# Small slots of the second expert stage: float32 weights without a split, products in separate columns of the array, loads in whole rows

## The chip, the cores and the metric

The kernel runs on one core of a Trainium2 chip. The metric is device time in microseconds from the first to the last instruction of that core. Three runs of the kernel before gave 2158.07 us in the median.

## What is computed

Two transformer blocks follow each other on 1024 tokens of 1024 features, in float32. Each has a mixer (a short convolution in the first, an mLSTM and a pooling branch in the second) and a layer of experts behind it. In the first block 16 experts take their 128 best tokens each. In the second block every token picks a group and, in it, two of eight experts; there are 32 experts of inner width 512. The change is about the products of these experts:

```python
def run_block(args):
    tok, e = args
    xb = hf[jnp.minimum(tok, n_tok - 1)]
    a = xb @ w_gate[e]                                # 1024 x 512
    b = xb @ w_up[e]                                  # 1024 x 512
    return (jax.nn.silu(a) * b) @ w_down[e]           # 512 x 1024
...
out = (out.reshape(n_slots, dm).astype(jnp.float32) * slot_gate[:, None]).astype(h.dtype)
y = jnp.zeros((n_tok, dm), h.dtype).at[slot_tok].add(out, mode='drop')
```

A final norm follows the second block.

## The kernel before

**Order of the kernel.** `block1` runs the first mixer, the routing and 16 experts; `block2` runs the second mixer, the routing, 32 expert slots and the final norm. In the profile the first expert stage lies at about 480 to 1030 us, the second mixer behind it, the second expert stage at about 1490 to 2131 us, and the final norm at the end.

**Slots of the second stage.** The routing sorts the 32 experts by their number of tokens into slots of four sizes: four slots of two blocks of 128 tokens (PAIRS_AT, positions 5, 10, 15, 20), twelve of 128 (the first three and WHOLE_AT), six of 64 (HALF_AT, positions 26 to 31) and ten of 32 (QUARTER_AT: 6, 7, 11, 12, 16, 17, 21, 22, 24, 25). The last two kinds are called small here; they have an entry "m", their number of tokens. Which expert a slot holds is read from memory by the SP queue when its weights are loaded.

**Order of the work.** `unit_order` gives, for slot after slot, the products of gate and up, the transposition of the next slot's tokens (xT), the products of the last slot's down, and the transposition of this slot's hidden values (hT). `queue_experts` loads the weights in the same order.

**Loads.** `Loader` runs chunks of 1 MB, [128, 4, 512] in float32, on the SP queue, four in flight, into 14 ring buffers (two rings of two, and two pools of five). A chunk covers 512 rows and 512 columns of a weight, by `chunk_src`. Where a weight is 512 wide (gate and up of the second stage) the pieces of 512 columns are whole rows of 2 KB; where it is 1024 wide (all weights of the first stage, down of the second) they are halves of rows.

**Splits.** TensorE multiplies in fp32r with operands split into hi and lo: ScalarE copies a rounded hi (L188) and VectorE subtracts it (L189). `ahead` in `run_experts` does so for half a chunk at a time (128 x 1024 numbers), into five split buffers, in the order of use. A chunk's ring buffer is free once its second half is split.

**Products of large slots** are three fp32r products for each block of 128 features (`mm3`, L196 to L198). **Small slots** turn their tokens so that hi and lo of xT lie side by side in the stationary columns (2m of them) and go once over the weights' hi (L554) and once over their lo (L555); the two halves of the result are added by `whole` (L560 and L561). Down's weights aren't split for small slots: hT is float32, and `product_few` multiplies the raw chunk (L552), one column half after the other. All these results begin at PSUM partition 0. The row product with the gate and the modulation row is L681; GpSimd then scatters the rows with an adding DMA (L515) to `acc_d`. GpSimd also gathers the tokens (L509).

**The end.** Slot 31's rows are not scattered: `keep_rows` keeps them, and the final norm adds them. Behind slot 30's scatter `load_sums` reads the sums back (L1336), and the final norm runs on them (L1402, L1415).

Of the kernel before, what the change touches and what calls it, by code (L numbers as in the profile page):

```python
# [21 lines left out]
P = 128  # L22
# [15 lines left out]
# positions of the slots where each kind starts, its tokens  # L38
# [12 lines left out]
class Loader:  # L51
    """Runs weight chunks from DRAM into rings of buffers, in the order of their use."""
# [13 lines left out]
    def drop_pools(self):  # L66
        """All but the first two."""
        del self.pools[2:]
# [24 lines left out]
            # what else wants the DMA engines doesn't wait behind more than this many loads  # L93
# [6 lines left out]

    def take(self, key):
        k, v, p = self.ready.popleft()
        assert k == key, (k, key)
        self.held[key] = p
        return v

    def done(self, key, keep=False):
        """keep: the buffer becomes the caller's, who takes it from the ring."""
        p = self.held.pop(key)
        if not keep:  # L110
            p[3] -= 1
            self.pump()
# [7 lines left out]
def kernel(ctx, tc, a, out):  # L120
# [13 lines left out]
    def psum_pools(stack, **bufs):  # L134
        """PSUM's 8 banks: mm and p tiles take two each, aux tiles one."""
# [9 lines left out]
    def keep_warm(n):  # L145
        """Products of constants while the tensor engine would wait for long, for its clock falls to half when idle."""
# [58 lines left out]
    C = {}  # L205

    def routing_consts():
# [10 lines left out]
        # before[s, t] = 1 where s < t  # L218
# [4 lines left out]
        # same[r, c] = 1 where r and c are the same modulo 16; prev: and r < c  # L223
# [6 lines left out]
        # the first token of each row's tile  # L230
# [15 lines left out]
    def turned_rows(pool, srcs):  # L246
        """Vectors as columns, in PSUM."""
# [8 lines left out]
    class Ada:  # L256
        """Columns of silu(c) @ ada_w + ada_b, 512 at a time; chunks of the weights run ahead."""
# [75 lines left out]
    def first_units(hls, ps, hT, ready):  # L333
        """The first few blocks of columns, by half of the tokens and feature block as they get ready."""
# [13 lines left out]
    def proj_T(hl, hT, n=P):  # L348
        """[n features, tokens] of h @ w for one block of columns; hT: its halves by token."""
# [15 lines left out]
    def mix_out(stack, b, y, parts, wo0, w_key, resid, g_row, mods, router, n_log, L, after_wo0, bias=None, ready=lambda tt: None, beside=lambda tt: None):  # L365
        """parts: y's feature blocks, those that get ready last behind; ready(tt): what is left to do for the last part;
        beside(tt): what else is to be done before the next tile;
        mods: scale, weight and shift of the second norm.
        L: the router's logits by token, (x * rstd * (1 + scale) * weight + shift) @ router with the columns' factors
        taken into the router and the tokens' left to the end."""  # L370
# [64 lines left out]
        for tt in range(NT):  # L435
# [29 lines left out]
            # the last tiles go ahead of the weights that follow  # L465
# [11 lines left out]
            if tt == NT - 1:  # L477
                # off the vector engine, which goes on with the routing
# [15 lines left out]
    class Experts:  # L494
# [34 lines left out]
        def transposed_few(self, x, n, tag, m):  # L529
            """Up to 64 tokens; xT: hi and lo side by side, for one pass over the weights' hi and one over their lo;  # L530
            hT: float32, for weights that are not split."""
# [3 lines left out]
            src = ps[:, :n * m].rearrange("p (k c) -> p k c", k=n)  # L535
# [12 lines left out]
        def product_few(self, sT, w, ps, ks, last):  # L548
            ps = ps[:sT.shape[2]]
            for i, k in enumerate(ks):  # L550
                if sT.dtype == F32:
                    nc.tensor.matmul(ps, sT[:, k], w[:, i], start=k == 0, stop=k == last)  # L552
                else:
                    nc.tensor.matmul(ps, sT[:, k], w[:, 0, i], start=k == 0, stop=False)  # L554
                    nc.tensor.matmul(ps, sT[:, k], w[:, 1, i], start=False, stop=k == last)  # L555

        def whole(self, t, p, m):
            """The sum of the halves that hi and lo give, kept in t."""
            t = t[:m]
            nc.scalar.copy(t, p[m:2 * m])  # L560
            nc.vector.tensor_tensor(t, p[:m], t, op=OP.add)  # L561
            return t
# [1384 lines left out]
```

## Time and profile before

| | us |
|---|---|
| three runs | 2157.3, 2158.07, 2159.38 |
| span of the profiled execution | 2157.5 |
| TensorE busy | 2007.7 (93%) |
| VectorE busy | 1653.2 (77%) |
| ScalarE busy | 1147.8 (53%) |
| GpSimd busy | 350.4 (16%) |

The profiled execution's own time is its span, from the first to the last instruction; nothing beside the span is listed for it. Busy time is the union of an engine's instructions. Consecutive matmuls overlap in the records, so a gap between two of them shows as idle only where it is longer than that overlap. The DMA share is the mean of the core's 16 DMA engines and can read slightly above 1.

### The profile page before, as it was taken

To read this page: it belongs to the slowest core of one execution; us is meant where nothing else is said; L and a number is where in the kernel's file an instruction comes from. 1 tells how busy PE (TensorE), PEld (TensorE's weight loads), DVE (VectorE), ACT (ScalarE), POOL (GpSimd) and SP (SyncE) were. 2 spreads that over 40 slices of the span, in tenths; PEclk is the share of its full clock that TensorE was granted. 3 is DMA by queue.
4 is the path that set the end of the run, shared out by engine and by line. 5 is a ranking of instruction groups with operands and counts; after the bars stand their busy time and mean duration, and the time that the engine had idled before them with its cause. 6 is when DMAs were issued, how large, how long until landed. Compare 5 with 4: busy or idle time off the path is not lost.

```text
span 2157.5 us, 25812 instructions
## 1 busy us (share of the span) xinstructions
PE 2007.7 (93%) x9192; PEld 1543.5 (72%) x9192; DVE 1653.2 (77%) x2073; ACT 1147.8 (53%) x1568; POOL 350.4 (16%) x300
## 2 busy tenths in 40 slices
PE   4999999949999999999699998996999999999997
PEld 3788878827888888888477877785886757575553
DVE  6699965458999999999562456777977787778886
ACT  4311122227777777777552444233766565656664
POOL 1054420040101010000100001004112121112210
PEclk7999999969999999999899999997999999999999
DMA  9467645389999999999502001538999999999996
GB/s 312 157 236 263 243 141 204 106 309 351 366 380 372 380 372 380 373 380 365 153 1 84 15 30 49 205 137 284 387 321 329 325 341 325 333 332 330 360 371 231
DMA packets 300799, 573.59 MB, mean 266 GB/s; under 512 B 30311, under 2 KB 53575, under 8 KB 300668
## 3 DMA queue, kind: packets, MB, share of 16 engines
q1 hardware_dynamic: 281116, 511.78, 66.2%
q0 software_dynamic: 19168, 59.46, 9.5%
q8 instruction: 73, 1.20, 0.2%
q10 hardware_dynamic: 384, 0.68, 0.1%
q14 instruction: 58, 0.48, 0.1%
HBM read 534.12 MB, written 42.66 MB: 267 GB/s over the span
## 4 chain that ended last, share of the span: by engine, by line
PE 85%; DVE 8%; ACT 3%; issue 2%; DMA 2%; POOL 0%; SPq 0%; DVEq 0%; ACTq 0%; POOLq 0%
PE mm L196 21%; PE mm L197 21%; PE mm L198 21%; PE mm L552 5%; PE aux L525 2%; PE mm L554 2%; PE mm L555 2%; DVE hl L189 2%; PE half L198 1%; PE half L196 1%; PE half L197 1%; PE aux L414 1%; ACT hl L188 1%; PE aux L1528 1%; DVE adacc L298 1%
## 5 line engine op out<-in xcount | busy, mean ns | idle before, releaser
L189 DVE TENSOR_TENSOR hl<-raw,hl 128x1024 fp32r<-128x1024 f32 x729 | 869.6, 1232 | 134.6 <-ACT hl L188 124.3
L188 ACT CAST hl<-raw 128x1024 fp32r<-128x1024 f32 x740 | 757.9, 1053 | 264.8 <-PE mm L198 226.9
L196 PE MATMUL mm<-hl,xT 128*128 128x512 f32 x832 | 330.9, 398 | 0.3 <-ACT xT L192 0.3
L198 PE MATMUL mm<-hl,xT 128*128 128x512 f32 x832 | 327.6, 394 | 0.0
L197 PE MATMUL mm<-hl,xT 128*128 128x512 f32 x832 | 327.6, 394 | 0.0
L196 PE MATMUL mm<-hT,hl 128*128 128x512 f32 x448 | 180.2, 402 | 8.2 <-ACT hT L819 5.9
L198 PEld LDWEIGHTS mm<-hl,xT 128*128 128x128 f32 x832 | 156.5, 188 | 36.7 <-DVE xT L193 0.7
L196 PEld LDWEIGHTS mm<-hl,xT 128*128 128x128 f32 x832 | 156.5, 188 | 35.5 <-ACT xT L192 0.8
L197 PEld LDWEIGHTS mm<-hl,xT 128*128 128x128 f32 x832 | 156.7, 188 | 34.6
L197 PE MATMUL mm<-hT,hl 128*128 128x512 f32 x448 | 178.6, 399 | 1.6 <-DVE hT L820 1.6
L198 PE MATMUL mm<-hT,hl 128*128 128x512 f32 x448 | 176.5, 394 | 0.0
L196 PE MATMUL mm<-hl,hT 128*128 128x512 f32 x416 | 168.4, 405 | 3.4 <-ACT hl L188 3.2
L197 PE MATMUL mm<-hl,hT 128*128 128x512 f32 x416 | 166.1, 399 | 3.8 <-DVE hl L189 3.8
L198 PE MATMUL mm<-hl,hT 128*128 128x512 f32 x416 | 165.8, 398 | 0.9 <-DVE hT L193 0.9
L552 PE MATMUL mm<-raw,hT 128*32 128x512 f32 (+1 forms) x256 | 113.0, 594 | 0.5 <-ACT hT L538 0.5
L515 POOL DMA_INDIRECT acc_d<-yo,idx x35 | 60.6, 1732 | 281.2 <-DVE yo L681 233.7
L196 PEld LDWEIGHTS mm<-hT,hl 128*128 128x128 f32 x448 | 85.7, 191 | 28.6 <-ACT hT L819 6.4
L554 PE MATMUL mm<-hl,xT 128*64 128x512 f32 (+1 forms) x256 | 101.6, 397 | 0.0
L555 PE MATMUL mm<-hl,xT 128*64 128x512 f32 (+1 forms) x256 | 101.0, 395 | 0.4 <-DVE hl L189 0.4
L298 DVE SCALAR_TENSOR_TENSOR adacc<-adaw,ccol,adacc 128x512 f32<-128x512 f32 x142 | 100.0, 770 | 0.0
L197 PEld LDWEIGHTS mm<-hT,hl 128*128 128x128 f32 x448 | 85.5, 191 | 19.3 <-DVE hT L820 2.4
L198 PEld LDWEIGHTS mm<-hT,hl 128*128 128x128 f32 x448 | 85.3, 190 | 19.1
(481 smaller groups left out, 3129.6 us busy)
## 6 DMA issues: line engine op xcount, KB each, us to landing
raw<-in_moe_w_gate_dram SPq DMA_DIRECT2D x64, 1024.0 KB
raw<-in_moe_w_up_dram SPq DMA_DIRECT2D x64, 1024.0 KB
raw<-in_moe_w_down_dram SPq DMA_DIRECT2D x64, 1024.0 KB
raw<-in_w_expert_gate_dram SPq DMA_DIRECT2D x64, 1024.0 KB
raw<-in_w_expert_down_dram SPq DMA_DIRECT2D x63, 1024.0 KB
raw<-in_w_expert_up_dram SPq DMA_DIRECT2D x62, 1024.0 KB
adaw<-in_ada_w_dram SPq DMA_DIRECT2D x47, 1024.0 KB
raw<-in_sc_w_in_dram SPq DMA_DIRECT2D x9, 1024.0 KB
```

The source lines that it names most:

```text
L188: nc.scalar.copy(hl[:, 0], raw)
L189: lo.tensor_tensor(hl[:, 1], raw, hl[:, 0].bitcast(F32), op=OP.subtract)
L196: nc.tensor.matmul(o, s_hi, m_hi, start=start, stop=False)
L197: nc.tensor.matmul(o, s_hi, m_lo, start=False, stop=False)
L198: nc.tensor.matmul(o, s_lo, m_hi, start=False, stop=stop)
L298: nc.vector.scalar_tensor_tensor(acc[kk % 2], w[:, k], c, add, op0=OP.mult, op1=OP.add)
L414: nc.tensor.matmul(o, xT[:, k], rsc[:, k], start=k == 0, stop=k == KC - 1)
L515: nc.gpsimd.indirect_dma_start(out=self.acc, out_offset=bass.IndirectOffsetOnAxis(ap=idx[:m], axis=0), in_=y[:m], in_offset=None, compute_ ...
L525: nc.tensor.transpose(ps[:, i * P:(i + 1) * P], x[:, k * P:(k + 1) * P], ident)
L552: nc.tensor.matmul(ps, sT[:, k], w[:, i], start=k == 0, stop=k == last)
L554: nc.tensor.matmul(ps, sT[:, k], w[:, 0, i], start=k == 0, stop=False)
L555: nc.tensor.matmul(ps, sT[:, k], w[:, 1, i], start=False, stop=k == last)
```

## The change

- For small slots of the second stage no weight is split any more. xT is float32 like hT, and gate and up are float32 products on the raw chunks. A chunk of gate stays in its ring buffer until the chunk of up with the same rows is there; `queue_experts` loads the two alternately.
- `product_few` places the products in the array. The first of its weights goes to the PSUM partitions from 0, the second to those from 64. For slots of 32 tokens odd feature blocks go 32 partitions higher than even ones. Its two weights are up and gate, or the two column halves of down.
- `few_sums` brings the parts together: for 64 tokens it copies the upper half down, for 32 it adds the two sums of each weight.
- `few` is the new path of small slots. It calls `ahead` for the weights of the next large slots, whose chunks may come later in the queue than the small ones'; `Loader.take` finds a chunk by its key, and `ahead` goes on only if that load has been issued.
- `chunk_src` loads whole rows in both expert stages: [128, 4, 512] for weights 512 wide, [128, 2, 1024] for weights 1024 wide. Large slots multiply the two column halves of a block of 128 features one after the other where the weight is 1024 wide; a pair's down then takes two PSUM tiles at once.

The diff also takes out comments, which are left out here.

```diff
+    def is_ready(self, key):
+        return any(r[0] == key for r in self.ready)
     def take(self, key):
-        k, v, p = self.ready.popleft()
-        assert k == key, (k, key)
+        i, (_, v, p) = next((i, r) for i, r in enumerate(self.ready) if r[0] == key)
+        del self.ready[i]
...
         def transposed_few(self, x, n, tag, m):
...
-            if tag == "hT":
-                t = self.tile("hT32", [n, P // 2], 1)[:, :, :m]
-                nc.scalar.copy(t, src)
-                return t
-            t = self.tile(tag, [2, n, P], self.wide, F32R).rearrange("p a b c -> p (a b) c")[:, :n, :2 * m]
-            nc.scalar.copy(t[:, :, 0:m], src)
-            nc.vector.tensor_tensor(t[:, :, m:], src, t[:, :, 0:m].bitcast(F32), op=OP.subtract)
+            t = self.tile(tag, [2, n, P], self.wide)[:, 0, :, :m]
+            nc.scalar.copy(t, ps[:, :n * m].rearrange("p (k c) -> p k c", k=n))
...
+        def product_few(self, sT, ws, ps, k, last):
+            m = sT.shape[2]
+            split = P // 2 // m
+            for i, w in enumerate(ws):
+                at = i * (P // 2) + k % split * m
+                nc.tensor.matmul(ps[at:at + m], sT[:, k], w, start=k < split, stop=k > last - split)
+        def few_sums(self, ps, m, outs):
+            if m == P // 2:
+                for i, o in enumerate(outs):
+                    if o is not None:
+                        nc.scalar.copy(o, ps[i * m:(i + 1) * m])
+                return
+            t = self.tile("whole", [512], 1)
+            for at in (P // 2, 0):
+                nc.scalar.copy(t[at:at + m], ps[at + m:at + 2 * m])
+            for i in (1, 0):
+                at = i * (P // 2)
+                nc.vector.tensor_tensor(outs[i], ps[at:at + m], t[at:at + m], op=OP.add)
...
+        def few(i, kind, c):
...
+            raw = ld.take(key)
+            if key[2] == "g":
+                gate_raw = key, raw
+                if ci == 0:
+                    ps = mm_ps()[:, 0]
+                return
+            if kind == "u":
+                for b in range(4):
+                    ex.product_few(s["xT"], (raw[:, b], gate_raw[1][:, b]), ps, ci * 4 + b, 7)
+                ld.done(gate_raw[0])
+            else:
...
+                for b in range(2):
+                    ex.product_few(s["hT"], [raw[:, b, h * 512:(h + 1) * 512] for h in range(2)], ps, ci * 2 + b, 3)
+            ld.done(key)
+            for _ in range(N_PARTS):
+                if len(hls) < N_SPLIT:
+                    ahead()
+            if ci < n_ch - 1:
+                return
+            if kind == "u":
+                s["hid"] = hid = ex.tile("hid", [fd], ex.wide)[:m]
+                if m == P // 2:
+                    nc.scalar.activation(hid, ps[m:], AF.Silu)
+                    nc.vector.tensor_tensor(hid, ps[:m], hid, op=OP.mult)
+                else:
+                    up = ex.tile("yo", [D], ex.wide)[:m, 0:fd]
+                    ex.few_sums(ps, m, (up, hid))
+                    nc.scalar.activation(hid, hid, AF.Silu)
+                    nc.vector.tensor_tensor(hid, up, hid, op=OP.mult)
+                return
...
+            y = ex.tile("yo", [D], ex.wide)
+            if m == P // 2:
+                ex.few_sums(ps, m, (None, y[:m, 512:]))
+                nc.vector.scalar_tensor_tensor(y[:m, :512], ps[:m], s["gate"][:m], ex.grow[:m, :512], op0=OP.mult, op1=OP.mult)
+                nc.vector.scalar_tensor_tensor(y[:m, 512:], y[:m, 512:], s["gate"][:m], ex.grow[:m, 512:], op0=OP.mult, op1=OP.mult)
...
+            ex.scatter(y, s["idx"], m)
...
-    def chunk_src(w, h, kg):
-        rows, cols = slice(kg * 512, (kg + 1) * 512), slice(h * 512, (h + 1) * 512)
+    def chunk_src(w, c, n):
+        rows = slice(c * P * 2048 // n, (c + 1) * P * 2048 // n)
...
-                ld.queue(key, [P, 4, 512], chunk_src(w, h, kg))
+                ld.queue(key, [P, 2048 // n, n], chunk_src(w, c, n))
...
+            if b["small"]:
+                b["u"] = [c for both in zip(b["g"], b["u"]) for c in both]
+                b["g"] = []
```

## Rows read from the trace of the kernel before

**Rows 1.** The page, part 2: busy tenths and bandwidth in 40 equal slices of the span.

```profile
PE   4999999949999999999699998996999999999997
PEclk7999999969999999999899999997999999999999
DMA  9467645389999999999502001538999999999996
GB/s 312 157 236 263 243 141 204 106 309 351 366 380 372 380 372 380 373 380 365 153 1 84 15 30 49 205 137 284 387 321 329 325 341 325 333 332 330 360 371 231
```

**Rows 2.** Windows of both expert stages; columns stand in the first line.

```profile
core 0: us, PE busy (x) PEld busy (x) DVE busy (x) ACT busy (x) POOL busy (x), PEclk, DMA share, GB/s
1500.00:2124.00 624.00, 609.69 (x2631) 416.49 (x2629) 501.47 (x501) 394.96 (x476) 107.34 (x71) 0.99 0.97 337
...
1520.00:1580.00 60.00, 60.00 (x284) 49.82 (x283) 58.21 (x58) 48.50 (x54) 7.90 (x6) 1.00 1.05 387
1600.00:1640.00 40.00, 38.57 (x173) 28.55 (x172) 30.08 (x32) 24.41 (x29) 3.70 (x3) 0.96 0.88 308
...
2040.00:2100.00 60.00, 60.00 (x233) 33.83 (x232) 50.93 (x51) 40.63 (x51) 8.56 (x7) 1.00 1.05 370
500.00:1020.00 520.00, 518.11 (x2350) 420.78 (x2349) 483.56 (x442) 406.83 (x427) 44.89 (x36) 1.00 1.05 373
```

**Rows 3.** Waits, 1500 to 2124 us: who waited for whom, total us, times, longest us.

```profile
POOL acc_d L515 <- DVE yo L681: 233.7, 29, 14.3
...
ACT hl L188 <- PE mm L198: 69.5, 103, 2.0
...
POOL acc_d L515 <- DMA acc_d<-yo,idx: 25.3, 4, 6.7
...
PEld mm L555 <- DVE hl L189: 9.1, 20, 0.8
```

**Rows 4.** Timeline of a small slot's gate and up, 1648.9 to 1649.3 us: start, duration.

```profile
1648.71 0.39 PE L555 MATMUL mm<-hl,xT 128*64 128x512 f32 x1
1648.94 0.40 PE L554 MATMUL mm<-hl,xT 128*64 128x512 f32 x1
...
1649.18 0.39 PE L555 MATMUL mm<-hl,xT 128*64 128x512 f32 x1
```

**Rows 5.** Chain of waits, one small slot's down: start, us on the chain, records.

```profile
1650.45 6.98 PE mm L552 x16
```

**Rows 6.** Groups by line and shape, 1500 to 2124 us: count, busy us, mean ns.

```profile
L189 DVE TENSOR_TENSOR hl<-raw,hl 128x1024 fp32r<-128x1024 f32 x316 | 375.1, 1229 | 68.1 <-ACT hl L188 64.5
L188 ACT CAST hl<-raw 128x1024 fp32r<-128x1024 f32 x315 | 318.0, 1052 | 70.7 <-PE mm L198 69.5 <-POOL hl L189 1.1
...
L552 PE MATMUL mm<-raw,hT 128*32 128x512 f32 x160 | 70.5, 594 | 0.0
...
L552 PE MATMUL mm<-raw,hT 128*64 128x512 f32 x80 | 35.4, 595 | 0.0
...
L552 PEld LDWEIGHTS mm<-raw,hT 128*32 128x32 f32 x160 | 16.8, 110 | 46.0 <-issue 45.9
...
L561 DVE TENSOR_TENSOR hid<-mm,hid 32x512 f32<-32x512 f32 x10 | 6.7, 671 | 0.0
L676 ACT ACTIVATE hid<-hid 32x512 f32<-32x512 f32 x10 | 6.3, 630 | 23.3 <-DVE hid L561 23.3
L560 ACT COPY hid<-mm 32x512 f32<-32x512 f32 x10 | 5.8, 579 | 0.2
```

**Rows 7.** DMA issues by tile, 1500 to 2124 us: count and size.

```profile
raw<-in_w_expert_down_dram SPq DMA_DIRECT2D x61, 1024.0 KB
```

**Rows 8.** Scatters to acc_d, 1500 to 2124 us: time from issue to landing.

```profile
DMA to landing us min/median/max: 4.4/7.0/13.2
```

**Rows 9.** Bandwidth in 40 slices of the kernel's first 20 us.

```profile
GB/s 0 0 0 8 8 131 0 418 401 393 451 418 401 410 418 418 393 418 401 389 389 393 381 381 389 385 389 389 389 385 389 381 389 389 385 389 389 389 381 385
```

**Rows 10.** Chain of waits, the end: start, us, what.

```profile
2117.45 7.03 PE mm L552 x16
2124.50 1.27 DVE yo L681
2126.05 4.38 DMA acc_d<-yo,idx
...
2133.05 7.23 DMA raw<-acc_d
```

More of the change, by code (lines that the diff above doesn't have):

```diff
@@ L580, in run_experts @@
             units += [(i, kind, c) for c in blocks[i][kind]] if kind in "gud" else [(i, kind, None)]
-        todo = deque((u[2][0], part) for u in units if u[2] is not None for part in range(N_PARTS))
+        todo = deque((u[2][0], part) for u in units if u[2] is not None and not blocks[u[0]].get("small") for part in range(N_PARTS))
         hls, raws = deque(), {}
-        whole = {b["g"][0][0][1] for b in blocks if b.get("small")}
         def ahead(lo=nc.vector):
-            if todo:
+            if todo and (todo[0][1] or ld.is_ready(todo[0][0])):
                 key, part = todo.popleft()
@@ L589, in ahead @@
                     raws[key] = ld.take(key)
-                raw = raws[key][:, part * KP:(part + 1) * KP]
-                if key[1] in whole and key[2] == "d":
-                    hls.append(raw)
-                    return
+                raw = raws[key]
+                raw = raw[:, part].rearrange("p (h f) -> p h f", h=2) if raw.shape[2] == D else raw[:, part * KP:(part + 1) * KP]
                 hl = hlp.tile([P, 2, KP, 512], F32R, tag="hl", name="hl")
@@ L642, in run_experts @@
                 continue
-            _, _, h, kg = c
-            kgs = (fd if kind == "d" else D) // 512
-            pair = len(bl) == 2
-            keep = bl[0].get("keep") if kind == "d" else None
-            if kg == 0 and (h == 0 or pair or keep):
-                ps = mm_ps()
+            if blocks[i].get("small"):
+                few(i, kind, c)
+                continue
+            _, _, ci, n_ch, width = c
+            kgs = (fd if kind == "d" else D) // P
+            if ci == 0:
+                if width == D:
+                    ps = [mm_ps() for _ in bl]
+                else:
+                    two = mm_ps()
+                    ps = [two[:, j:j + 1] for j in range(len(bl))]
             for part in range(N_PARTS):
@@ L652, in run_experts @@
                 hl = hls.popleft()
-                ks = range(kg * 4 + part * KP, kg * 4 + (part + 1) * KP)
                 for j, s in enumerate(bl):
-                    product = ex.product_few if "m" in s else ex.product
-                    product(s["hT" if kind == "d" else "xT"], hl, ps[:, j if pair else h], ks, kgs * 4 - 1)
-            if kind == "d" and i in whole:
-                ld.done(c[0])
-            if keep:
-                keep(ps[:, h], bl[0], h)
-                continue
@@ L662, in run_experts @@
-            if kg < kgs - 1 or not (pair or h == (D if kind == "d" else fd) // 512 - 1):
+                    sT = s["hT" if kind == "d" else "xT"]
+                    if width == D:
+                        for h in range(2):
+                            ex.product(sT, hl[:, :, h:h + 1], ps[j][:, h], [ci * 2 + part], kgs - 1)
+                    else:
+                        ex.product(sT, hl, ps[j][:, 0], range(ci * 4 + part * KP, ci * 4 + (part + 1) * KP), kgs - 1)
+            if ci < n_ch - 1:
@@ L663, in run_experts @@
                 continue
             for j, s in enumerate(bl):
-                m = s.get("m", P)
-                p = ps[:, j] if pair else ps.rearrange("p a b -> p (a b)")[:, :D if kind == "d" else fd]
+                p = ps[j].rearrange("p a b -> p (a b)")
                 if kind == "g":
-                    s["hid"] = t = ex.tile("hid", [fd], ex.wide)
+                    s["hid"] = ex.tile("hid", [fd], ex.wide)
+                    nc.scalar.activation(s["hid"], p, AF.Silu)
                 elif kind == "u":
-                    t = ex.tile("whole", [fd], 1) if "m" in s else None
-                elif not pair or h == 0:
-                    s["y"] = t = ex.tile("yo", [D], ex.wide)
@@ L673, in run_experts @@
[L673 to L686 removed]
+                    nc.vector.tensor_tensor(s["hid"], p, s["hid"], op=OP.mult)
+                else:
+                    y = ex.tile("yo", [D], ex.wide)
+                    nc.vector.scalar_tensor_tensor(y, p, s["gate"], ex.grow, op0=OP.mult, op1=OP.mult)
+                    ex.scatter(y, s["idx"])
+                    if "after" in s:
+                        s["after"]()
```

55 lines of the change are left out of this document (23 added, 32 removed).

## The prediction

> **What bounds the kernel now.** I began with the page's slices [rows 1]: the change touches the weights of both expert stages, which are the two long runs of nines in the DMA line. One table of windows then puts the stages side by side [rows 2]. In the first stage (500 to 1020 us) TensorE is busy 518.11 of 520 us, and the DMA share stands at 1.05. In the second (1500 to 2124) TensorE is busy 609.69 of 624 us, but the share is only 0.97 at 337 GB/s. The same table shows what a saturated share looks like: 1.05, at 387 GB/s where weights alone move (1520 to 1580), 370 where gathers and scatters mix in (2040 to 2100). So the second stage keeps its DMA engines at 0.97/1.05 = 92% of what they can do. TensorE decides, and DMA has some 47 us of slack in 624: 624 x (1 - 0.97/1.05).
>
> The waits of that stretch agree [rows 3]: the hi half of the splits (L188) waits 69.5 us for TensorE to free a split buffer, and no engine but GpSimd, whose scatters and gathers wait for one another, waits long for a DMA. The splits are ahead of TensorE and the loads ahead of the splits. That the DMA sits so close behind is the fact on which the forecast rests: making TensorE faster can give back 47 us at most, plus what the loads themselves get quicker.
>
> **What a small slot costs now.** There are 16: ten of 32 tokens (QUARTER_AT), six of 64 (HALF_AT). Gate and up are 8 feature blocks x 2 weights x 2 halves (hi, lo) = 32 fp32r products, 512 in all 16 slots; starts in a timeline are 0.23 us apart [rows 4], so 7.3 us a slot, 117 us in all. Down is 8 float32 products whose 16 records take 6.98 us [rows 5]: 0.436 us a record, two records a product, 0.873 us a product, 112 us in all. Records of 32 columns last as long as those of 64, 594 and 595 ns [rows 6]: a narrow stationary tile by itself saves nothing.
>
> **The change, part by part.**
>
> *Gate and up unsplit.* Per slot 16 float32 products take the place of 32 fp32r ones. One after the other they would take 16 x 0.873 = 14.0 us, 6.7 more than now. The gain lies only in the placing: gate's result goes to PSUM partitions from 64 on, up's below, and at 32 tokens odd and even feature blocks get quarters of their own. No row of this trace has two products at once in different columns, so the price is bounded: 14.0 us with no overlap, 3.5 with four abreast. I take half, 7.0 us. Each float32 product is two records, each with its own weight load (160 loads for the 80 products of the quarter slots), for the same columns [rows 6]. If records start in order, the second record of a product can run only beside the first of the next, whatever the number of column groups; that makes one product per 0.436 us at 32 and 64 tokens alike. Change: 117 to 112 us in all.
>
> *Down's column halves side by side.* By the same reckoning 112 becomes 56 us (bounds 112 and 28-56).
>
> *TensorE's sum.* 610 - 5 - 56 = 549 us.
>
> The Trainium skill, "TensorEngine Tiling (Array Packing)", Theoretical Speedup, gives up to 2x for a dimension of at most 64 and up to 4x for 32; by it the ten quarter slots would take 16 x 0.218 + 8 x 0.218 = 5.2 us instead of 10.5, and TensorE 52 us less still. The rows on narrow records neither confirm nor refute that. Since DMA decides below, the forecast would not move by it.
>
> *Splits.* 16 slots x 8 pieces = 128 pieces no longer pass L188 and L189 (1.05 and 1.23 us each [rows 6]): 135 us off ScalarE, 157 off VectorE. Neither engine is the limit; these hide under the products and are worth nothing beyond the short TensorE waits on L189 in [rows 3] (9.1 us on weight loads). `few_sums` adds per quarter slot four copies and four additions where there were two and two, 0.58 and 0.68 us a piece [rows 6]. Half of these stand between the last gate and up product and hT: with silu and the product of the two (0.63 and 0.68) some 4 us, beside the next xT and the last down, 0.6 + 3.5 us. That hides them, and where a cover shrinks (four abreast) TensorE waits 1 to 2 us a slot, inside the time that DMA sets.
>
> *Added waits.* `up` of a quarter slot takes a "yo" buffer, so the second quarter behind a pair waits until a scatter of the pair has landed, 7.0 us in the median [rows 8]. Queued behind it on VectorE are hid and the next splits, and hT on TensorE waits: at most 3 us at four places, and nothing if DMA decides. `ahead` inside `few` puts a split of the next large slot, whose load is some seven chunks further on, into ScalarE's queue in front of this slot's sums. TensorE then idles until that chunk lands. It costs time only if the 14 buffers are full meanwhile; 7 are held then, so loading goes on.
>
> *Whole rows.* Gate and up here are 512 wide, so their loads were whole rows already. Only down's (61 chunks in the stretch, [rows 7]) go from 2 KB to 4 KB pieces, and all of the first stage's. The first loads of the kernel show the rates: x_tok in rows of 4 KB at 393 to 451 GB/s, mean 412, then ada's weights in 2 KB pieces at 381 to 389 [rows 9]. A chunk of 1.049 MB takes 2.55 instead of 2.71 us: 61 x 0.165 = 10 us less DMA. Bounds: 0, if gathers eat it, and 16 us at 430 GB/s. The first stage gets none: TensorE idles 1.9 us in 520 there [rows 2], and its products stay as many and as long. SP issues the same number of loads. Fewer pieces cost it no more.
>
> *What is late next.* TensorE needs 549 us plus the 14 it idles now. DMA needs 624 x 0.97/1.05 = 576, less 10 = 566. DMA decides. Not all of its slack can be had: in the first pair (1600 to 1640, share 0.88 [rows 2]) the rings are full before any small slot has run, so 40 x (1 - 0.88/1.05) = 6.5 us stay idle, and I leave 3 more for stretches at a lower granted clock (0.99 in the mean now [rows 2]) and for the start. Gain: 47 - 9.5 + 10 = 47.5 us.
>
> The Trainium skill, "DMA: Bandwidth & Descriptors", Specifications, lists an HBM limit of about 358 GB/s per core. The trace differs: 387 GB/s over 60 us in [rows 2], so the measurement decides. By the page's figure the stretch's 210 MB (337 GB/s x 624 us) would take 587 us, an estimate, and the gain would be 37.
>
> *The end.* The chain runs from slot 30's down (2117.45) over its row product, its scatter (4.38 us) and the reload of the sums (7.23) to the final norm [rows 10]. After the change that down ends 3.5 us sooner behind its weights, but ScalarE's copy of the upper half (0.58) and a second row product (two halves where one of 1.27 stood) come after it: about 1 us more. Sum: -46.5 us.
>
> The profiled execution spans 2157.5 us and stands 0.6 below the median of 2158.07; the forecast is 2158 - 46.5, rounded to **2111 us**.
>
> **The rivals.**
>
> *No overlap, slower than before.* If float32 products in different columns still run one by one, gate and up cost 16 x 14.0 = 223 us instead of 117: TensorE goes from 610 to 716 and decides alone. Price 106 us, less up to 8 of the idle time: about 2260 us. The point from which it turns is the overlap factor at which 384 products of 0.873 us cost today's 229 us: 335/229 = 1.46. For it: no row shows an overlap, and a record's length does not depend on its columns. Against it: the products name distinct columns and partitions, and the moving data of a record needs 0.436 us for 512 columns where fp32r takes 0.23, so the array is not fed at its fastest. The Trainium skill, "TensorE: Matmul & The Clock Gate", Part 3, reports 2.38x for three column tiles, which no run here shows yet. Chance 0.16.
>
> *Partial overlap, 1.25 to 1.6.* TensorE lands between 335/1.6 = 209 and 335/1.25 = 268 us for these products (229 now) and stays the limit or level with DMA: from -25 us, with the shorter waits on splits, to +25; 2133 to 2183 us. Chance 0.09.
>
> *DMA gives nothing back.* The share of 0.97 might already be all that a mix with scatters allows (the landing of scatters is up to 13.2 us [rows 8]); then only the 4 KB rows and the tail help: -5 to -15, 2143 to 2153 us. Against it: 1.05 in 2040 to 2100 with gathers and scatters running. Chance 0.05.
>
> *The forecast's case.* DMA decides from the second group of slots to the end: 2095 (4 KB rows at their best, all slack taken but the first pair's) to 2132 (no gain from rows, a quarter of the slack lost to a clock that falls while TensorE waits). Chance 0.70.
>
> **How the numbers follow.** No change means within 0.2%, some 4 us, about what a measurement of this kernel can tell from none. Faster takes the forecast's case, the third rival and half of the second: 0.77; same 0.04; slower 0.19. The range 2093 to 2160 holds the first and third cases and half of the second, about 0.78. Within the likeliest case alone it is 2095 to 2132.
>
> **What would show it.** Right: starts of `product_few` 0.44 us apart in pairs that overlap, a DMA share near 1.05 from 1700 us to the end of the loads, TensorE idle in the quarter slots with loads of w_expert as the releaser, 4 KB pieces for down, a first stage as long as before. Wrong: records of the new products 0.436 us apart with no two at once (first rival); a share still under 1.0 with TensorE waiting on hid or hT (the added waits); 4 KB loads no quicker than 387 GB/s (the 10 us fall away); a granted clock at its lower level through the last six slots, which would put 12 us of products per slot at twice their length.

## The result and the profile after

The changed kernel takes 2109.56 us in the median of four runs (2108.81 to 2113.6); the kernel before, measured beside it, takes 2158.73. The ratio is 0.9776, with a 95% interval of 0.9764 to 0.9787: 48 us less. The profiled execution spans 2111.6 us, 45.9 less than the one before; it is the slowest of the four, and a span lies some 2 us below the time of its run (2111.6 for 2113.6), so spans are compared only with spans.

The page's slices, where [rows 1] stood:

```profile
PE   4999999949999999999879999898799889898776
PEclk7999999969999999999979999999799999999988
DMA  9467746288999999999432011426899999999997
GB/s 319 144 234 260 257 145 226 104 292 309 378 377 394 382 393 380 394 373 381 124 106 80 11 35 36 160 110 242 303 391 296 380 358 369 373 371 355 360 368 298
```

From the 32nd to the 39th slice the bandwidth now stands at 355 to 380 GB/s where it stood at 325 to 371, and the PE line has sevens and eights in it: TensorE waits there, and the DMA engines hardly do. The windows of both stages, columns as in [rows 2]:

```profile
core 0: us, PE busy (x) PEld busy (x) DVE busy (x) ACT busy (x) POOL busy (x), PEclk, DMA share, GB/s
1520.00:1580.00 60.00, 60.00 (x284) 49.85 (x283) 58.33 (x57) 48.54 (x55) 7.94 (x6) 1.00 1.04 392
1600.00:1640.00 40.00, 40.00 (x233) 28.21 (x235) 24.87 (x25) 19.37 (x25) 5.28 (x4) 1.00 0.88 299
1640.00:2060.00 420.00, 363.07 (x1884) 239.16 (x1876) 236.13 (x248) 187.61 (x247) 68.12 (x52) 0.93 1.03 366
500.00:1020.00 520.00, 518.12 (x2343) 420.81 (x2342) 482.22 (x441) 405.82 (x426) 44.89 (x36) 1.00 1.00 375
```

In the kernel before, the stretch from 1640 to 2060 us read:

```profile
1640.00:2060.00 420.00, 409.97 (x1754) 271.74 (x1753) 331.19 (x334) 259.71 (x316) 79.02 (x49) 0.99 0.97 335
```

From 1640 us on the share is 1.03, against 1.04 in the stretch where weights alone move (1520 to 1580): the DMA engines are full, and TensorE is busy 363 of 420 us, at a granted clock of 0.93 in the mean. In the first pair (1600 to 1640) the share is 0.88, as before. The first stage is what it was, 518 of 520 us of TensorE. The groups by shape of the second stage (1495 to 2085 us) answer to [rows 6]:

```profile
L551 PE MATMUL mm<-raw,xT 128*64 128x512 f32 x192 | 54.5, 720 | 29.4 <-DMA raw<-in_w_expert_up_dram 29.4
L551 PE MATMUL mm<-raw,xT 128*32 128x512 f32 x320 | 36.4, 595 | 0.0
L551 PE MATMUL mm<-raw,hT 128*64 128x512 f32 x96 | 22.1, 598 | 0.8 <-ACT hT L538 0.7
L551 PE MATMUL mm<-raw,hT 128*32 128x512 f32 x160 | 19.5, 600 | 0.1
L192 DVE TENSOR_TENSOR hl<-raw,hl 128x1024 fp32r<-128x1024 f32 x188 | 227.3, 1237 | 82.1 <-ACT hl L191 79.4
L191 ACT CAST hl<-raw 128x1024 fp32r<-128x1024 f32 x188 | 195.5, 1053 | 92.4 <-PE mm L201 81.7 <-DMA raw<-in_w_expert_gate_dram 8.1 <-DMA raw<-in_w_expert_down_dram 2.2
L565 DVE TENSOR_TENSOR yo<-mm,whole 32x512 f32<-32x512 f32 x30 | 20.4, 681 | 25.1 <-DMA acc_d<-yo,idx 21.8 <-ACT whole L562 2.5
```

The splits went from 316 to 188. The ten quarter slots spend 36.4 us on gate and up, 3.64 a slot, and 19.5 on down, 1.95 a slot; one record still lasts 595 ns, so the gain is all in how many run at once. The weight loads show it. A timeline of the load line in a quarter slot:

```profile
1730.75 0.13 PEld L551 LDWEIGHTS mm<-raw,xT 128*32 128x32 f32 x4 [0.30 <-issue]
1731.18 0.13 PEld L551 LDWEIGHTS mm<-raw,xT 128*32 128x32 f32 x4 [0.30 <-issue]
1731.61 0.13 PEld L551 LDWEIGHTS mm<-raw,xT 128*32 128x32 f32 x4 [0.30 <-issue]
```

Four loads come together every 0.43 us: four records at once, each in its own quarter. The Trainium skill, "TensorEngine Tiling (Array Packing)", Theoretical Speedup, gives up to 4x at 32; the trace agrees, with 3.64 us a slot against the 13.92 that the same products take one by one (experiment below), 3.8 times less.

The waits of the second stage (1495 to 2080 us), the five that bear on the forecast:

```profile
PE mm L551 <- DMA raw<-in_w_expert_up_dram: 29.4, 11, 7.0
...
PE aux L536 <- DVE xT L196: 24.1, 4, 6.7
...
DVE yo L565 <- DMA acc_d<-yo,idx: 21.8, 5, 5.1
...
PEld mm L551 <- DMA raw<-in_w_expert_up_dram: 9.8, 7, 2.0
...
ACT hl L191 <- DMA raw<-in_w_expert_gate_dram: 8.1, 3, 5.0
```

TensorE waits for chunks of up, for which nothing waited before. By the groups above, all 29.4 us of it lie in the slots of 64 tokens. The lines of L565 and L191 are the two added waits of the forecast: VectorE for a "yo" buffer, and a split called ahead for a chunk not yet there. The wait for "yo" reaches TensorE, as one of four places shows:

```profile
1834.12 0.68 DVE L565 TENSOR_TENSOR yo<-mm,whole 32x512 f32<-32x512 f32 x1 [4.82 <-DMA acc_d<-yo,idx]
...
1834.90 0.68 DVE L671 TENSOR_TENSOR hid<-yo,hid 32x512 f32<-32x512 f32 x1
...
1836.24 0.63 PE L536 MATMUL aux<-ident,hid 32*128 32x32 f32 x4 [6.09 <-DVE xT L196]
```

The addition into `up` waits until a scatter has landed, hid comes behind it, and the transposition of hid (L536) finds TensorE idle for 6.09 us. The releaser that the profile names, a split of xT, stands behind hid in the same queue of VectorE. At four places this makes 24.1 us. Slot 30's down and row products, and its scatter, against [rows 10]:

```profile
2073.18 3.60 PE L551 MATMUL mm<-raw,hT 128*64 128x512 f32 x16
...
2077.45 0.74 DVE L682 SCALAR_TENSOR_TENSOR yo<-mm,gate,grow 64x512 f32<-64x512 f32 x1 [2.74 <-ACT yo L558]
2078.11 0.73 DVE L683 SCALAR_TENSOR_TENSOR yo<-yo,gate,grow 64x512 f32<-64x512 f32 x1
...
2079.13 1.41 POOL L518 DMA_INDIRECT acc_d<-yo,idx  x1 [14.84 <-DVE whole L1409]
```

The scatter is issued 46.9 us earlier than before (2079.13 for 2126.05), and the span ends 45.9 us earlier. Slot 30's down itself ends 47.7 us earlier (2076.78 for 2124.48): 0.8 us of that go to the copy and the second row product in front of the scatter, and 1.0 between the scatter and the end. So the whole gain is there when the last slots end.

### The profile page after: what moved, and what is told of

Read it like the earlier page. It is cut to its first block, busy times and chain, and to the rows that moved or that the text cites. A ratio compares the mean times of both kernels' runs of the same rounds, so it can differ in the third digit from the quotient of the medians.

```text
span 2111.6 us, 25403 instructions
## 1 busy us (share of the span) xinstructions
PE 1908.3 (90%) x9192; PEld 1477.3 (70%) x9192; DVE 1506.1 (71%) x1934; ACT 1035.9 (49%) x1454; POOL 334.8 (16%) x300
## 2 busy tenths in 40 slices
DMA packets 235516, 573.56 MB, mean 272 GB/s; under 512 B 30311, under 2 KB 53575, under 8 KB 235388
## 5 line engine op out<-in xcount | busy, mean ns | idle before, releaser
L192 DVE TENSOR_TENSOR hl<-raw,hl 128x1024 fp32r<-128x1024 f32 x601 | 721.9, 1234 | 149.6 <-ACT hl L191 145.2
L191 ACT CAST hl<-raw 128x1024 fp32r<-128x1024 f32 x612 | 634.5, 1053 | 287.8 <-PE mm L201 240.7
L199 PE MATMUL mm<-hl,xT 128*128 128x512 f32 x832 | 335.2, 403 | 0.3 <-ACT xT L195 0.3
L201 PE MATMUL mm<-hl,xT 128*128 128x512 f32 x832 | 331.1, 398 | 0.0
L200 PE MATMUL mm<-hl,xT 128*128 128x512 f32 x832 | 331.1, 398 | 0.0
L201 PEld LDWEIGHTS mm<-hl,xT 128*128 128x128 f32 x832 | 158.7, 191 | 37.5 <-DVE xT L196 0.7
L199 PEld LDWEIGHTS mm<-hl,xT 128*128 128x128 f32 x832 | 159.2, 191 | 36.3 <-ACT xT L195 0.8
L200 PEld LDWEIGHTS mm<-hl,xT 128*128 128x128 f32 x832 | 159.2, 191 | 35.5
L199 PE MATMUL mm<-hl,hT 128*128 128x512 f32 x416 | 166.5, 400 | 0.2 <-ACT hT L195 0.2
L201 PE MATMUL mm<-hl,hT 128*128 128x512 f32 x416 | 163.8, 394 | 0.9 <-DVE hT L196 0.9
L200 PE MATMUL mm<-hl,hT 128*128 128x512 f32 x416 | 163.6, 393 | 0.0
L551 PE MATMUL mm<-raw,xT 128*32 128x512 f32 (+1 forms) x512 | 90.9, 642 | 29.4 <-DMA raw<-in_w_expert_up_dram 29.4
L518 POOL DMA_INDIRECT acc_d<-yo,idx x35 | 54.7, 1562 | 274.8 <-DVE yo L736 123.2
L201 PEld LDWEIGHTS mm<-hl,hT 128*128 128x128 f32 x416 | 78.1, 188 | 19.4 <-DVE hT L196 1.4
L199 PEld LDWEIGHTS mm<-hl,hT 128*128 128x128 f32 x416 | 78.1, 188 | 17.4 <-ACT hT L195 0.5
```

Source lines behind the costliest of these rows:

```text
L191: nc.scalar.copy(hl[:, 0], raw)
L192: lo.tensor_tensor(hl[:, 1], raw, hl[:, 0].bitcast(F32), op=OP.subtract)
L199: nc.tensor.matmul(o, s_hi, m_hi, start=start, stop=False)
L200: nc.tensor.matmul(o, s_hi, m_lo, start=False, stop=False)
L201: nc.tensor.matmul(o, s_lo, m_hi, start=False, stop=stop)
L518: nc.gpsimd.indirect_dma_start(out=self.acc, out_offset=bass.IndirectOffsetOnAxis(ap=idx[:m], axis=0), in_=y[:m], in_offset=None, compute_ ...
```

## The experiments

**Theory D** is the forecast's case: in the changed kernel the loads decide from the second group of small slots to the end, and TensorE's sum, the splits and the added waits lie beside them. Its rivals are that TensorE still decides, that the added waits do, or that the time came from the whole rows alone; each expectation names what it sets against D. The first four kernels below vary the changed kernel, and their pages are set against it. The versions that follow look for what is left.

**One by one.** All products of small slots stand at partition 0, the two weights in two PSUM banks; the sums of quarters go.

```diff
-                at = i * (P // 2) + k % split * m
-                nc.tensor.matmul(ps[at:at + m], sT[:, k], w, start=k < split, stop=k > last - split)
+                nc.tensor.matmul(ps[:m, i], sT[:, k], w, start=k == 0, stop=k == last)
```

> The changed kernel, but all float32 products of small slots give results from PSUM partition 0 on, in two banks, so none can stand beside another in the array; the sums behind them need fewer operations. If the overlap makes the gain: 384 products at 0.873 us one after the other, TensorE some 716 us in the stage, 2250 to 2270 us, slower than the kernel before. If fewer splits or whole rows made it: 2110 to 2150.

It took 2247.26 us, 1.041 of the kernel before (1.0391 to 1.0429), a little below what was expected. Its groups and its window:

```profile
L549 PE MATMUL mm<-raw,xT 128*32 128x512 f32 x320 | 139.2, 593 | 0.0
L549 PE MATMUL mm<-raw,xT 128*64 128x512 f32 x192 | 83.7, 594 | 0.0
...
1640.00:2060.00 420.00, 415.89 (x1600) 243.21 (x1599) 207.24 (x209) 162.42 (x202) 55.81 (x44) 1.00 0.89 302
```

Gate and up cost 139.2 us in the quarter slots, 13.9 each, where four abreast cost 36.4. TensorE is full and the DMA share falls to 0.89. The first rival's mechanism is thus real, and the placing in the array is worth 138 us (2247.26 less 2109.56). Without it the change would have lost 89.

**Two abreast.** Quarter slots are placed as those of 64 tokens are, up below and gate from 64 on; the additions, the copies for them and the use of "yo" by up go too.

```diff
-                at = i * (P // 2) + k % split * m
-                nc.tensor.matmul(ps[at:at + m], sT[:, k], w, start=k < split, stop=k > last - split)
+                at = i * (P // 2)
+                nc.tensor.matmul(ps[at:at + m], sT[:, k], w, start=k == 0, stop=k == last)
```

> The changed kernel, but slots of 32 tokens place only two products side by side (columns from 0 and from 64), as those of 64 do, and odd and even blocks add up in the same place; the sums behind them are one copy. TensorE gets some 52 us more work in the ten quarter slots, where it now idles. Theory D: no change within 3 us, 2107 to 2113. Theory P, or any theory by which four abreast is what gained: 2125 to 2160.

2110.93 us, ratio 0.9779 (0.9766 to 0.9792): the changed kernel's time. A group and the window:

```profile
L550 PE MATMUL mm<-raw,xT 128*32 128x512 f32 x320 | 70.6, 594 | 0.0
...
1640.00:2060.00 420.00, 400.07 (x1918) 244.41 (x1914) 213.47 (x221) 173.26 (x223) 68.07 (x52) 0.98 1.03 367
```

TensorE works 37 us more in this stretch (400.07 for 363.07), at a granted clock of 0.98 for 0.93, and the DMA share is 1.03 in both. The 24.1 us of waits at L536 are gone from this run's waits, and TensorE waits for up 18.2 us in place of 29.4. So the quarters, the waits for "yo" that go with them and the lower clock, taken away together, don't move the time of the changed kernel; what each alone would do, this run doesn't tell. Its quarter slots cost 106.9 us of TensorE (70.6 here and 36.3 for down), where the forecast had 105: on TensorE, this is the kernel that the forecast priced.

**Fewer bytes.** Small slots load half of gate and up.

```diff
-                b["u"] = [c for both in zip(b["g"], b["u"]) for c in both]
+                b["u"] = [b["g"][0], b["u"][0]]
...
-                for b in range(4):
-                    ex.product_few(s["xT"], (raw[:, b], gate_raw[1][:, b]), ps, ci * 4 + b, 7)
+                for b in range(8):
+                    ex.product_few(s["xT"], (raw[:, b % 4], gate_raw[1][:, b % 4]), ps, b, 7)
```

> The changed kernel, but small slots load only the first half of gate and up and use it twice, with as many products as before: the second halves of these weights are left out of the computation. 32 chunks less, some 87 us of DMA work. Theory D: DMA falls below TensorE's 509 us, which then sets the stage with its waits, 2055 to 2070 us. Theory P: the waits stay, 2100 to 2112 us.

2058.27 us, ratio 0.9535 (0.952 to 0.9549): another 51 us less, with as many products. The group that waited for chunks of up in the changed kernel:

```profile
L551 PE MATMUL mm<-raw,xT 128*64 128x512 f32 x192 | 42.5, 595 | 0.0
```

It waits no more, and costs 42.5 us instead of 54.5; without waits six slots cost 7.1 us each, two abreast. The expectation holds, and with it D: fewer bytes are less time. But of some 87 us of loads only 51 came. TensorE is now busy 498 of 524 us (1500 to 2024), and the loads stand still for want of a buffer: from 1495 us on SP waits 235.9 us for splits to free one, where it waited 87.9 in the changed kernel.

**Half rows.** The same chunks, but one that is 1024 wide comes by two loads, in pieces of 2 KB.

```diff
+            if shape[-1] == D:
+                first = (engine or self.nc.sync).dma_start(v[:, :, 0:512], s_ap[:, :, 0:512]).ins
...
+                ins = (engine or self.nc.sync).dma_start(v[:, :, 512:1024], s_ap[:, :, 512:1024]).ins
```

> The changed kernel, but every chunk of a weight 1024 wide is fetched by two loads of 512 columns, so in pieces of 2 KB again; same chunks, same order, same products. Theory D (after the change the DMA engines set the second expert stage): 61 chunks of down at some 0.16 us more, so 8 to 14 us more than the changed kernel, 2118 to 2124 us, with a DMA share at its ceiling to the end of the loads and a first expert stage as long as before. Theory R (the gain came mostly from the whole rows): back near 2140 to 2158. Theory P (waits of TensorE on hid and hT set the stage): no change, 2108 to 2113.

2117.83 us, ratio 0.981 (0.9797 to 0.9824): by the ratios 7 us of the changed kernel's gain go, by the medians 8. Its windows:

```profile
1640.00:2060.00 420.00, 356.94 (x1848) 237.28 (x1842) 234.96 (x246) 185.83 (x245) 68.27 (x52) 0.93 1.04 361
...
500.00:1020.00 520.00, 518.11 (x2343) 421.07 (x2342) 482.33 (x441) 406.00 (x426) 44.94 (x36) 1.00 1.05 373
```

With the DMA engines as full, 361 GB/s move instead of 366. The first stage has its old share of 1.05 back and the same time. Whether the second load of a chunk costs something by itself, this run doesn't tell apart from its smaller pieces.

**Rows only.** The other half alone: the kernel before with chunks in whole rows, small slots split as before.

```diff
-                ld.queue(key, [P, 4, 512], chunk_src(w, h, kg))
+                ld.queue(key, [P, 2048 // n, n], chunk_src(w, c, n))
...
+                    for h in range(2):
+                        nc.tensor.matmul(ps[:m, h], s["hT"][:, k], hl[:, h * 512:(h + 1) * 512], start=k == 0, stop=k == 3)
```

> The kernel before with the whole-row loads alone: small slots split gate and up into hi and lo as before, one product after the other, and down goes over both column halves of each block of 128 features. Theory D says that TensorE sets the stage here, so cheaper loads only raise the DMA's slack: 2154 to 2159 us against 2158 of the kernel before, with a DMA share in the second expert stage some 0.02 lower. Theory R, that rows gain wherever they are: 2148 us or less.

2161.53 us, ratio 1.0013 (1.0004 to 1.0022): not a gain but 2 to 3 us of loss, which neither theory had expected. The DMA share of the stage (1500 to 2124 us) goes from 0.97 to 0.96. Window, VectorE's timeline of the last slot's two row products, and behind it the first of the two in the kernel before:

```profile
1640.00:2060.00 420.00, 409.93 (x1755) 271.98 (x1754) 330.49 (x328) 259.75 (x316) 72.92 (x49) 0.99 0.97 335
...
2132.98 0.74 DVE L1405 SCALAR_TENSOR_TENSOR yo<-mm,gate,grow 64x512 f32<-64x512 f32 x1 [4.97 <-PE mm L654]
...
2135.11 0.74 DVE L1405 SCALAR_TENSOR_TENSOR yo<-mm,gate,grow 64x512 f32<-64x512 f32 x1
```

```profile
2129.05 0.74 DVE L1363 SCALAR_TENSOR_TENSOR yo<-mm,gate,grow 64x512 f32<-64x512 f32 x1 [1.53 <-PE mm L552]
```

TensorE is as full as before and the loads wait for it, so quicker loads are worth nothing. Where the loss may come from: with whole-row chunks a column half of down isn't complete before the last chunk, so the first row product of the last slot comes 4 us later than in the kernel before.

**Rows only, halves in turn.** As the last, but the last slot keeps its chunks and takes all products of the first column half ahead of those of the second.

```diff
+                    for k, hl in enumerate(lasts):
+                        nc.tensor.matmul(ps[:m, h], s["hT"][:, k], hl[:, h * 512:(h + 1) * 512], start=k == 0, stop=k == 3)
                     s["keep"](ps[:, h], s, h)
```

> This is the kernel before with whole-row loads alone, as in the run with rows only, but in the last slot's down all products of the first column half stand before those of the second again. In the run with rows only the last slot's first row product started at 2132.98 us where the kernel before had 2129.05, its second at 2135.11 instead of 2132.49, and the norm's first addition at 2139.14 instead of 2136.53. Theory K (keep): with whole-row chunks both column halves of the last slot come out at the same time, and that alone made the run with rows only 2 to 3 us longer; then this kernel comes back to the kernel before, 2157 to 2160 us, with the last slot's two row products some 3.5 us apart. Rival: the loss lies elsewhere (in the loads or in the first stage), and this kernel stays at 2161 to 2163 us.

2157.85 us, ratio 0.9998 (0.9989 to 1.0007), and the row products:

```profile
2128.00 0.74 DVE L1413 SCALAR_TENSOR_TENSOR yo<-mm,gate,grow 64x512 f32<-64x512 f32 x1 [1.53 <-PE mm L675]
...
2132.49 0.74 DVE L1413 SCALAR_TENSOR_TENSOR yo<-mm,gate,grow 64x512 f32<-64x512 f32 x1 [2.37 <-PE mm L675]
```

Theory K holds, and whole rows alone are worth nothing: what they give in the changed kernel (at most some 7 to 8 us, if the second load of a chunk costs nothing by itself) appears only once the loads decide.

**Small slots early.** In the first pair the loads idle (share 0.88), because the ring buffers are full before any small slot has run: from 1595 to 1640 us SP waits 24.3 us for splits to free one. Two quarter slots go ahead of it.

```diff
-QUARTER_AT = (6,7,11,12,16,17,21,22,25,24)
+QUARTER_AT = (3,4,11,12,16,17,21,22,25,24)
```

> The changed kernel with the first two slots of 32 tokens at positions 3 and 4 in place of 6 and 7, ahead of the first pair, so that the rings don't fill before TensorE has run small slots. Theory D: the 6 us that the DMA engines stand still at 1600 to 1640 us are used, 2102 to 2106 us. If those were not on the path that sets the end: 2109 to 2112.

2107.91 us, ratio 0.9757 (0.9744 to 0.977): outside both ranges. It is 4 us less by the ratios and 1.6 by the medians, and the interval overlaps that of the changed kernel, so this run alone shows no gain. The idle time is gone from its old place:

```profile
1600.00:1640.00 40.00, 40.00 (x199) 32.71 (x188) 35.56 (x38) 28.32 (x34) 7.91 (x6) 1.00 1.04 383
```

**No empty rows.** A slot's places without a token gather a row all the same. From the third slot on the gathers use the scatters' list, which skips them.

```diff
-                    b["subs"] = [dict(src=r["src"][:, c:c + 1], idx=r["idx"][:, c:c + 1], gate=r["gate"][:, c:c + 1]) for c in cols]
+                    b["subs"] = [dict(src=r["idx" if s > 1 else "src"][:, c:c + 1], idx=r["idx"][:, c:c + 1], gate=r["gate"][:, c:c + 1]) for c in cols]
```

> The changed kernel, but from slot 2 on the gathers skip places without a token instead of fetching the first row for them; what such a place computes is weighed with 0 and scattered nowhere, as before. Some 1100 of 3264 gathered rows of 4 KB fall away, 4.5 MB. Theory D: less work for the DMA engines is less time, 5 to 11 us, 2099 to 2105. Theory P: no change, 2108 to 2112.

2107.89 us, ratio 0.9768 (0.9754 to 0.9781): no difference that can be told, and a miss. The page counts 569.57 MB instead of 573.56. At the 366 GB/s of the stretch those 4.0 MB would be 11 us; some 2 came, by the ratios and by the medians, too little to tell from none. In the first pair the loads idle a little more:

```profile
1600.00:1640.00 40.00, 39.60 (x234) 27.13 (x232) 24.54 (x24) 20.07 (x28) 5.29 (x4) 1.00 0.85 292
```

Most of what the gathers leave is lost to full buffers: from 1495 us on SP waits 107.7 us for splits to free one, where it waited 87.9. Summed over slices of 20 us from 1500 to 2040 us, with 1.04 as the full share, the loads stand still for 9.4 us in the changed kernel and for 16.5 here, by this estimate from the windows 7 us more; 14.0 of the 16.5 lie before 1720 us, in and around the first two pairs:

```profile
1500.00:1720.00 220.00, 209.10 (x1062) 163.77 (x1061) 173.05 (x171) 139.56 (x168) 38.26 (x29) 0.98 1.00 360
```

```profile
1500.00:1720.00 220.00, 209.09 (x1062) 163.70 (x1061) 172.79 (x172) 139.66 (x169) 36.90 (x28) 0.98 0.97 351
```

The first line is the changed kernel's, the second this run's. With small slots early the same sum is 5.6 us: 3.8 of the 9.4 are gone, not 6, for the loads now idle more in the second pair (0.87 for 0.95 from 1700 to 1720 us).

**Both.** The two edits together.

> Both: small slots at positions 3 and 4, and no gather of empty places. Theory D: the two savings of DMA time add up, 2092 to 2100 us.

2102.51 us, ratio 0.9736 (0.9723 to 0.9749). The interval lies below that of the changed kernel: this version beats both kernels, by 9 us the changed one (0.9776 less 0.9736), though less than was expected. The loads stand still for 11.5 us by the sum above; 2.1 more than in the changed kernel, against 11 us of bytes saved, agrees with the 9.

**Both, two abreast.** Does the finding on quarters hold in this version?

> This is the fastest version so far (two small slots early, empty places not gathered) with the slots of 32 tokens only two abreast, so that a slot's TensorE time rises by some 5 us and the waits for a yo buffer and the sums of quarters go. Theory D: loads still decide, so it takes the same time as with four abreast, 2100 to 2105 us, with the granted clock nearer to full speed (0.98 or more from 1640 to 2060 us). Rival T: with fewer bytes and no idle first pair TensorE is close to the limit, and 10 times 5 us show, at least in part: 2107 us or more. Rival Y: the waits for yo buffers did cost time: 2099 us or less.

2107.84 us, ratio 0.9764 (0.9751 to 0.9778): 6 us slower by the ratios, with intervals apart. D's expectation missed in the time, though the granted clock is 0.99 from 1640 to 2060 us, as expected; the time is in rival T's range. The windows of this version, then the first one's counterpart with four abreast:

```profile
1600.00:1640.00 40.00, 40.00 (x195) 31.28 (x194) 33.09 (x34) 25.95 (x31) 6.82 (x5) 1.00 0.94 320
1640.00:1840.00 200.00, 197.26 (x947) 140.13 (x945) 136.00 (x136) 107.22 (x129) 29.91 (x23) 1.00 1.00 349
```

```profile
1600.00:1640.00 40.00, 40.00 (x198) 32.70 (x191) 35.56 (x38) 28.33 (x34) 8.29 (x6) 1.00 1.02 362
```

Two abreast TensorE is busy 197 of 200 us behind the first pair, but so it was in the changed kernel with two abreast, at no cost in time. What differs stands in the first lines: in the first pair the loads fall from 1.02 back to 0.94. Over 1500 to 2040 us they stand still for 15.8 us where it was 11.5 with four abreast, and from 1590 to 1720 us SP waits 81.4 us for splits to free a buffer where it waited 40.9. By these rows the loads still set the time, and slower quarter slots ahead of the first pair cost it by leaving the buffers full: that accounts for 4 of the 5 to 6 us. Rival T, by which TensorE's own time shows, is neither proved nor needed for them.

A tile of its own for `up`, instead of a "yo" buffer, wasn't tried, so what the wait for "yo" costs by itself is not shown.

## Why the prediction was right

- **DMA decides** held. The forecast took 47 us of slack from two shares, 0.97 and 1.05; the changed kernel fills it (1.03 in 1640 to 2060), and the runs with fewer bytes and with half rows show that the loads now set the time. In the forecast's own sum the two engines lay only 3 us apart (563 and 566), so the margin was thin there; the run with two abreast, which costs TensorE what the forecast said, shows that the loads decide all the same.
- **Gate and up unsplit, 64 tokens**: 0.436 us a product was forecast, 7.0 a slot; 7.1 was measured where nothing waits (fewer bytes). The half price was right there.
- **Quarter slots**: this step failed. "If records start in order, the second record of a product can run only beside the first of the next, whatever the number of column groups" gave 7.0 us for a slot's gate and up and 3.5 for its down; 3.64 and 1.95 were measured, 0.228 us a product. The two records of a product don't hold up the other groups. With 55.9 us for ten slots where the forecast had 105, TensorE needs 49 us less than its 549, at full clock and without waits. The estimate by the Trainium skill, "TensorEngine Tiling (Array Packing)", Theoretical Speedup, in the prediction (52 us less) was the better price. It didn't move the forecast, as it said, and the two-abreast run shows that.
- **Whole rows**: 10 us were forecast; half rows cost 7 to 8, within the bounds 0 and 16, and part of that may be the second load of each chunk. The condition proved essential: alone, they give nothing.
- **Idle time of the loads**: the forecast left 9.5 us, 6.5 of them in the first pair, and 9.4 were left (the estimate under "No empty rows"). In the first pair the share stayed at 0.88. The other 3 us were meant for the clock and the start; they lie mostly in the second pair (0.95 from 1700 to 1720 us). The run that fills the first pair gained 2 to 4 us, not clear of noise.
- **Clock**: the granted clock fell to 0.93 in the mean. It is 0.72 from 1830 to 1842 us, a mean of its two levels (1.2 and 2.4 GHz), where TensorE had been idle for 6.09 us, and 0.90 from 1980 to 2078 us, among the waits for up; two abreast it is 0.98, and the time is the same. The sign of being wrong that the prediction gives for the last six slots has a slip: by its own prices a slot there is 10.5 us of products, not 12.
- **Added waits**: the yo wait came at five places and up to 5.1 us. The forecast had hT on TensorE wait at most 3 us at four places; it waited at four, 5.3 to 6.7 us each and 24.1 in all. The split called ahead waited for gate three times, up to 5.0. The first lies beside the loads: the run without it is no faster. No run takes the second away.
- **A sign that didn't come**: TensorE was to idle in the quarter slots with loads as the releaser. There it idles for hid, as said; for loads it idles in the slots of 64 tokens. And the sign of being wrong, waits on hid or hT with a share under 1.0, came by half: the waits did, at a share of 1.03.
- **The first stage** is unchanged, as forecast: 518.12 us for 518.11.
- **The end**: slot 30's down takes 3.60 us instead of 7.03, and the copy (L558) and the second row product stand behind it as listed. They cost 0.8 us where the forecast had about 1. Another 1.0 us is lost behind the scatter, for which the forecast had no term.
- **The rivals**: "no overlap" forecast 2260 us for a mechanism that costs 2247.26 when it is brought about; the 106 us of TensorE were right, and it fell only because the array does overlap. "Partial overlap" fell too: the 335 us of these products one by one became 120.5 (36.4, 19.5, 22.1 and, without waits, 42.5), a factor of 2.8. "DMA gives nothing back" fell with the share of 1.03.

The parts, 47.5 and -1, thus come near the measured 48 by a sum whose terms on the path were each near: what was left idle, the rows, the end. Those that were far off, the price of the quarter slots and the waits on hid, lay beside the loads, as the forecast had said of both. The 0.6 us that the prediction sees between a span and the median sets two measures side by side that lie some 2 us apart; nothing rests on it.

## What to carry to other kernels

When one engine is full and another stands at 92% of its saturated rate, price a change to the first by the second's slack, read in the same stretch: beyond it, making the first engine faster buys nothing, and a saving for the second is worth something only after the first has been relieved (whole rows: 0 us alone, up to 7 to 8 behind the placing), and then only as far as free buffers let its loads run on (gathers: some 2 of 11 us). Small stationary operands should be placed side by side in the array: products one by one cost 3.8 times as much here. When a layout of chunks changes, look at the last unit of the kernel, where what used to come out in two steps may now come out in one (2 to 3 us).

## What was not expected of the hardware

- Four float32 products of 32 columns run at once, though each is two records with a load of its own: 0.228 us a product, 0.44 for two abreast, 0.87 alone.
- The DMA share in the first stage fell from 1.05 to 1.00 with whole rows while 375 GB/s moved instead of 373; with the half rows it went back to 1.05. The same weights in pieces of 4 KB thus take less of the engines' time; "full" is 1.03 to 1.04 in the changed kernel where it was 1.05, and a share is to be compared within one kernel.
- Weights alone moved at 392 GB/s for 60 us (1520 to 1580). The Trainium skill, "DMA: Bandwidth & Descriptors", Specifications, lists about 358 GB/s per core for HBM, as half of what two cores share; here one core runs, and what it moves with the other busy no run shows. The measurement decides: by the page's figure the gain would be 37 us, an estimate, instead of 48.
- Gathers that skip 4.0 MB of rows saved some 2 us, not the 11 of their bytes: in this kernel the loads then stood still 7 us longer for full buffers.
